# The row of -M of each head is written to DRAM and read back by transfers that GpSimd issues instead of SyncE

## The chip, the cores and the metric

The kernel runs on one core of one Trainium2 chip. The metric is the device time of one execution in microseconds (us). The profile names the engines PE (TensorE), PEld (its weight loads), DVE (VectorE), ACT (ScalarE), POOL (GpSimd) and SP (SyncE, which only issues transfers here). Its page shows two queues for the kernel's own transfers: q1, "hardware_dynamic", and q0, "software_dynamic". The transfers that SP issues run on the first, those that POOL issues on the second.

## The reference

One decoder layer on a sequence of 256 tokens and 1024 channels, in float32. A combined projection feeds two branches, an mLSTM branch (4 heads of 256) and an attention branch (8 heads of 128 with a relative position bias). The gated sum of both goes through an output projection, a LayerNorm, a convolutional gated MLP and a second LayerNorm. What matters here is the mLSTM branch, which weighs the scores of a head by exponentials that a running maximum keeps in range:

```python
log_f = jax.nn.log_sigmoid(f_pre.astype(jnp.float32))
b_cum = jnp.cumsum(chunks(log_f), axis=-1)
...
d_intra = jnp.where(causal, b_c[..., :, None] - b_c[..., None, :] + li_c[..., None, :], -jnp.inf)
m_q = jnp.maximum(inter, d_intra.max(-1))
...
s = jnp.einsum("bhld,bhsd->bhls", q_c, k_c) * jnp.exp(d_intra - m_q[..., None])
num = w_inter[..., None] * jnp.einsum("bhld,bhde->bhle", q_c, C) + jnp.einsum("bhls,bhse->bhle", s, v_c)
```

The kernel treats all 256 tokens as one chunk. With F the running sum of the log forget gates, G = (input gate) - F and M the running maximum of G, the weight of key s for query l is exp(G[s] - M[l]). G[s] is one number per partition there, and M[l] a row that all 128 partitions need.

## The kernel before

All weights pass through as 81 chunks of 1 MB (`order`). A chunk is loaded by SP into one of three `raw` buffers (line 94). ACT casts it to the high half `wh` (line 99), DVE takes the difference as the low half `wl` (line 100), and TensorE forms each product from three matmuls on the halves (lines 130 to 132). Step s of the loop in `run` first does the elementwise work of the step before and splits chunk s+2 (`elem_work`), then issues the load of chunk s+5, then the matmuls of chunk s, and then the small matmuls of the heads (`side_pe`). Every engine executes its instructions in the order in which this program issues them, and SP and POOL issue transfers in that order too: a transfer that has to wait holds back all that stands behind it on its engine.

Four groups g of eight steps each (qm, qb, km, kb, vm, vb, ga, gb) hold one mLSTM head and two attention heads. The gates of all four heads are worked out once, in group 0 (`gates_schedule`). At its end `e1d` puts -M of the four heads into `nM` (4 partitions of 256 numbers) and writes it to the DRAM tile `mrows`. In each group `row_m` reads the row of its head back to all 128 partitions, as `nMb`. The exponentials of `el_w` (lines 643 and 644, on ACT) read `nMb`; POOL then zeroes what is not causal (line 645), `el_s` multiplies with the scores and splits the product into `sph` (line 656, ACT) and `spl` (line 662, DVE), and `pe_n` multiplies these with the values into `psn`. In the table of the group's steps `row_m` stands in step 4, `el_w` in step 6 and `pe_n` behind the matmuls of step 6 (3, 5 and 5 in the last group).

POOL also issues the transfers of the attention bias. The table of biases is written to DRAM once (line 542). For each group `copy_band` (line 377) spreads two rows of it to a `band` in DRAM and `load_band` (line 382) reads that back, shifted by one number per partition, as `toe`.

Of the kernel before, what the change touches and what calls it, by code (L numbers as in the profile page):

```python
# [18 lines left out]
P = 128  # L19
S = 256  # L20
# [58 lines left out]
class Kernel:  # L79
# [469 lines left out]
    def gates_schedule(self, bif):  # L549
        nc, mp = self.nc, self.xp  # L550
        st = {}
        v = nc.vector

        def e0():
            gt = mp.tile([P, 2, 8], F32, name="gt")
            for t in range(2):
                v.tensor_add(gt[:, t, :], self.psg[t][:, 256:264], bif)
            st["gt"] = gt

        def p0():  # L560
            ps = self.ps_side([4, 2, S], "ps_gt")
            for w in range(2):
                for t in range(2):
                    nc.tensor.transpose(ps[:, w, t * P:(t + 1) * P], st["gt"][:, t, 4 * w:4 * w + 4], self.ident)
            st["ps"] = ps

        def e1():
            ps = st["ps"]
            big = mp.tile([P, KT, S], F32, tag="xraw", name="gates")
            fs, t1, F, G, M, nFM, nM = (big[0:4, k, :] for k in range(7))  # L570
            v.tensor_copy(fs, ps[:, 1, :])
            v.scalar_tensor_tensor(t1, fs, -1.0, fs, op0=ALU.mult, op1=ALU.min)
            nc.scalar.activation(t1, t1, AF.Exp)
            nc.scalar.activation(t1, t1, AF.Ln, bias=1.0)
            st["g"] = fs, t1, F, G, M, nFM, nM

        def e1b():
            fs, t1, F, G, M, nFM, nM = st["g"]
            one = self.ones4[:, 0:S]
            v.scalar_tensor_tensor(fs, fs, 0.0, t1, op0=ALU.min, op1=ALU.subtract)  # L580
            v.tensor_tensor_scan(F, one, fs, 0.0, op0=ALU.mult, op1=ALU.add)

        def e1c():
            fs, t1, F, G, M, nFM, nM = st["g"]
            v.tensor_sub(G, st["ps"][:, 0, :], F)
            v.tensor_tensor_scan(M, self.ones4[:, S:2 * S], G, 0.0, op0=ALU.max, op1=ALU.max)

        def e1d():
            fs, t1, F, G, M, nFM, nM = st["g"]
            v.tensor_scalar(self.nM[0:4, :], M, -1.0, None, op0=ALU.mult)  # L590
            v.scalar_tensor_tensor(nFM, F, -1.0, M, op0=ALU.mult, op1=ALU.subtract)
            st.update(G=G, nFM=nFM)
            nc.sync.dma_start(self.mrows, self.nM[0:4, :])

        def p1():
            ps = self.ps_side([P, 2, 2, 4], "ps_gc")
            for w, n in enumerate(("G", "nFM")):
                for t in range(2):
                    nc.tensor.transpose(ps[:, w, t, :], st[n][:, t * P:(t + 1) * P], self.ident[0:4, 0:4])
            st["gc"] = ps  # L600

        def e2():
            self.gcol = self.const.tile([P, 2, 4], F32, name="gcol")
            self.floor = self.const.tile([P, 2, 4], F32, name="floor")
            nc.scalar.copy(self.gcol, st["gc"][:, 0])
            self.floor_exp = lambda: nc.scalar.activation(self.floor, st["gc"][:, 1], AF.Exp)

        b = self.start_g[0]
        self.gate_sums = e0
        self.side_pe.setdefault(b, []).append(p0)  # L610
        self.mixed[b + 1] = lambda w: w[0:1] + [None, None] + w[1:] + [e1]
        self.mixed[b + 2] = lambda w: w + [e1b, None, e1c, None, e1d]
        self.side_pe.setdefault(b + 5, []).append(p1)
        self.gate_cols = e2


    def group_schedule(self, g):
        nc = self.nc
# [2 lines left out]
        b = self.start_g[g]  # L621

        def row_m():
            nc.sync.dma_start(self.nMb, self.mrows[g:g + 1, :].to_broadcast([P, S]))

        def pe_s():
            qh, ql = self.hl["qm"]
# [176 lines left out]

        o = int(g < NG - 1)
        at(self.side_elem, 3 + o, row_m)
        at(self.side_pe, 4 + o, pe_s)
        at(self.side_pe, 4 + o, lambda: pe_l(0))
# [411 lines left out]
```

## Time and profile before

| what | value |
|---|---|
| median of 3 runs | 487.28 us (487.03 to 487.93) |
| profiled execution, its own time | 487.25 us |
| span of its profile | 485.5 us (1.75 us lie around it) |
| PE busy | 476.1 us, 98% of the span |
| DVE, ACT, POOL busy | 76%, 59%, 6% |
| queue of SP (q1) | 87.61 MB, 50.7% of 16 DMA engines' span |
| queue of POOL (q0) | 6.07 MB, 3.8% |

Times in the profile count from the start of the span. A row of the timeline or of the chain begins with the start and the duration in us. The chain is followed back from the last instruction: at each step to what released it. A row of a wait reads "engine line waited for: us in total, times, longest". A row on a transfer ends with the us from its issue to its landing (the median, where it stands for several).

### The profile page before, as it was taken

The page shows a single profiled execution, that of the slowest core. Times are in us where ns is not written, and L with a number is a line of the kernel's source. Part 1 is how long each engine was busy: PE and PEld are TensorE (multiplying, and loading weights), DVE is VectorE, ACT ScalarE, POOL GpSimd, SP SyncE. Part 2 cuts the span into 40 slices and gives each one's busy share as a digit, 9 for nine tenths or more (in the row PEclk, how much of TensorE's full clock was granted, in tenths as well). Part 3 has the DMA queues.
Part 4 walks back from the last instruction along what each step waited for, and adds up shares of the span by engine and source line. Part 5 has one row for each costly group of instructions (what it writes and reads, how often), then busy time and mean ns, then how long its engine had stood idle before and what let it go on. Part 6 is the DMA issues. An engine that isn't in the chain of part 4 may idle for free.

```text
span 485.5 us, 9409 instructions
## 1 busy us (share of the span) xinstructions
PE 476.1 (98%) x3832; PEld 460.4 (95%) x3832; DVE 369.7 (76%) x674; ACT 287.1 (59%) x492; POOL 28.0 (6%) x43
## 2 busy tenths in 40 slices
PE   8999999999999999999999999999999999999993
PEld 6999999999999999999999999999999999999983
DVE  4877976797689668986677788888668666866877
ACT  5568775686667756866654622767456544654530
POOL 0501011001100110002000001000000000000000
PEclk9999999999999999999999999999999999999998
DMA  7985676375636552743954581727564655455202
GB/s 220 323 297 165 234 250 199 110 259 199 215 102 258 191 211 88 270 175 104 381 211 173 177 344 50 298 88 261 174 217 172 210 184 198 165 217 200 88 1 88
DMA packets 20918, 94.29 MB, mean 194 GB/s; under 512 B 4837, under 2 KB 7793, under 8 KB 11017
## 3 DMA queue, kind: packets, MB, share of 16 engines
q1 hardware_dynamic: 16714, 87.61, 50.7%
q0 software_dynamic: 4160, 6.07, 3.8%
q8 instruction: 30, 0.49, 0.4%
q14 instruction: 14, 0.11, 0.1%
HBM read 92.58 MB, written 2.64 MB: 196 GB/s over the span
## 4 chain that ended last, share of the span: by engine, by line
PE 84%; DMA 6%; DVE 6%; ACT 2%; issue 1%; SPq 1%; DVEq 0%; ACTq 0%
PE ps_up L132 8%; PE ps_up L131 8%; PE ps_up L130 8%; PE ffn L132 4%; PE ffn L131 4%; PE ffn L130 4%; DMA raw<-in_wst_dram 3%; DVE wl L100 3%; DMA nMb<-mrows 2%; PE mix L130 2%; PE ps_wa L131 2%; PE ps_wb L131 2%; PE ps_gb L132 1%; PE ps_gb L130 1%; PE ps_gb L131 1%; PE mix L132 1%
## 5 line engine op out<-in xcount | busy, mean ns | idle before, releaser
L100 DVE TENSOR_TENSOR wl<-raw,wh 128x1024 fp32r<-128x1024 f32 (+3 forms) x158 | 180.6, 1184 | 28.0 <-ACT wh L99 27.3
L99 ACT CAST wh<-raw 128x1024 fp32r<-128x1024 f32 (+3 forms) x158 | 152.5, 1018 | 9.2 <-DMA raw<-in_wst_dram 6.5
L132 PE MATMUL ps_up<-x1h,wl 128*128 128x256 f32 x320 | 88.6, 277 | 0.0
L130 PE MATMUL ps_up<-x1h,wh 128*128 128x256 f32 x320 | 88.6, 277 | 0.0
L131 PE MATMUL ps_up<-x1l,wh 128*128 128x256 f32 x320 | 88.5, 277 | 0.0
L131 PEld LDWEIGHTS ps_up<-x1l,wh 128*128 128x128 f32 x320 | 60.1, 188 | 0.4
L130 PEld LDWEIGHTS ps_up<-x1h,wh 128*128 128x128 f32 x320 | 60.1, 188 | 0.3
L132 PEld LDWEIGHTS ps_up<-x1h,wl 128*128 128x128 f32 x320 | 60.1, 188 | 0.0
L1045 DVE SCALAR_TENSOR_TENSOR cu<-ps_up,vec,cu 128x255 f32<-128x255 f32 (+1 forms) x80 | 33.0, 475 | 23.5 <-ACT cu L1041 23.5
L132 PE MATMUL ffn<-wh,hl 128*128 128x512 f32 (+1 forms) x94 | 35.5, 378 | 0.0
L131 PE MATMUL ffn<-wl,hh 128*128 128x512 f32 (+1 forms) x94 | 35.5, 377 | 0.0
L130 PE MATMUL ffn<-wh,hh 128*128 128x512 f32 (+1 forms) x94 | 35.3, 375 | 0.0
L99 ACT CAST hh<-cu 128x256 fp32r<-128x256 f32 x22 | 8.9, 406 | 42.9 <-DVE cu L1053 42.9
L1041 ACT ACTIVATE cu<-ps_up,vec 128x256 f32<-128x256 f32 x40 | 16.7, 468 | 26.1 <-PE ps_up L132 26.1
L132 PEld LDWEIGHTS ffn<-wh,hl 128*128 128x128 f32 x94 | 17.7, 188 | 3.2
L131 PEld LDWEIGHTS ffn<-wl,hh 128*128 128x128 f32 x94 | 17.7, 188 | 3.1
L130 PEld LDWEIGHTS ffn<-wh,hh 128*128 128x128 f32 x94 | 17.7, 188 | 3.0
L130 PE MATMUL ps_ga<-xth,wh 128*128 128x256 f32 x64 | 18.2, 284 | 0.0
L130 PE MATMUL ps_qm<-xth,wh 128*128 128x256 f32 x64 | 18.1, 282 | 0.0
L132 PE MATMUL ps_ga<-xth,wl 128*128 128x256 f32 x64 | 17.9, 280 | 0.0
L131 PE MATMUL ps_ga<-xtl,wh 128*128 128x256 f32 x64 | 17.9, 280 | 0.0
L130 PE MATMUL mix<-wh,mgh 128*128 128x256 f32 x64 | 17.9, 279 | 0.0
(319 smaller groups left out, 1438.7 us busy)
## 6 DMA issues: line engine op xcount, KB each, us to landing
raw<-in_wst_dram SPq DMA_DIRECT2D x77, 1024.0 KB, 4.9
raw<-in_wst_dram SPq DMA_DIRECT2D x8, 256.0 KB, 4.5
lnrow<-in_rows_dram POOLq DMA_DIRECT2D x4, 512.0 KB, 6.9
band<-table POOLq DMA_DIRECT2D x4, 384.0 KB, 13.5
xraw<-in_xt_dram SPq DMA_DIRECT2D x8, 128.0 KB, 3.9
toe<-band POOLq DMA_DIRECT2D x4, 256.0 KB, 4.8
xtok<-in_x_dram POOLq DMA_DIRECT2D x1, 1024.0 KB, 7.7
sgb<-in_wst_dram SPq DMA_DIRECT2D x4, 128.0 KB, 3.9
```

Of the source, the lines that this page charges most:

```text
L99: self.nc.scalar.copy(wh, raw)
L100: self.nc.vector.tensor_sub(wl, raw, wh.bitcast(F32))
L130: mm(ps, ah if first is None else first, bh, start=start, stop=False)
L131: mm(ps, ah, bl, start=False, stop=False)
L132: mm(ps, al, bh, start=False, stop=stop)
L1041: act.activation(cu[:, j, :], ps[:, j, :], AF.Copy, scale=tap(2, j))
L1045: v.scalar_tensor_tensor(cu[:, j, o:], ps[:, j, :S - o], tap(t, j), cu[:, j, o:], op0=ALU.mult, op1=ALU.add)
```

## The change

Two lines change: the write of `mrows` in `e1d` and the read of `nMb` in `row_m` are issued by POOL in place of SP. That is one write of 4 KB and four reads that each fill 128 KB. Where they stand in the program stays the same.

```diff
@@ -590,7 +590,7 @@
             v.tensor_scalar(self.nM[0:4, :], M, -1.0, None, op0=ALU.mult)
             v.scalar_tensor_tensor(nFM, F, -1.0, M, op0=ALU.mult, op1=ALU.subtract)
             st.update(G=G, nFM=nFM)
-            nc.sync.dma_start(self.mrows, self.nM[0:4, :])
+            nc.gpsimd.dma_start(self.mrows, self.nM[0:4, :])
 
@@ -621,7 +621,7 @@
         def row_m():
-            nc.sync.dma_start(self.nMb, self.mrows[g:g + 1, :].to_broadcast([P, S]))
+            nc.gpsimd.dma_start(self.nMb, self.mrows[g:g + 1, :].to_broadcast([P, S]))
```

The order on PE, DVE and ACT is the same. On POOL, this is what stands in group 0 between the first `toe` and the first causal selection (`wt_882` is the tile of weights of head 0):

```order
 L377 DMA band_411<-table 256x1x384
 L382 DMA toe<-band_411 128x2x256
+L593 DMA mrows<-nM 4x256
+L624 DMA nMb<-mrows 128x256
 L645 AFFINE_SELECT wt_882<-wt_882 128x256
 L377 DMA band_412<-table 256x1x384
```

The write and the first read now stand directly behind the load of `toe`, which itself waits for the band.

On POOL in group 1 (the other groups are alike; `scl_990` is a scale of head 0):

```order
 L704 TENSOR_TENSOR scl_990<-scl_990,mhalf 128x2
 L382 DMA toe<-band_412 128x2x256
+L624 DMA nMb<-mrows 128x256
 L645 AFFINE_SELECT wt_1513<-wt_1513 128x256
 L377 DMA band_413<-table 256x1x384
```

The read of the next head's row now follows the next `toe`.

On SP in group 0, where the `raw` are the weight chunks:

```order
 L94 DMA raw_447<-in_wst_dram 128x2048
 L94 DMA raw_529<-in_wst_dram 128x2048
-L593 DMA mrows<-nM 4x256
 L94 DMA raw_599<-in_wst_dram 128x2048
 L94 DMA raw_672<-in_wst_dram 128x2048
-L624 DMA nMb<-mrows 128x256
 L94 DMA raw_736<-in_wst_dram 128x2048
 L94 DMA raw_797<-in_wst_dram 128x2048
```

The write leaves its place two chunks ahead of the read, and the read its place behind chunk `raw_672`.

## Rows read from the trace of the kernel before

**Rows 1.** The page: the span, and TensorE's busy time.
```profile
span 485.5 us, 9409 instructions
PE 476.1 (98%) x3832; PEld 460.4 (95%) x3832; DVE 369.7 (76%) x674; ACT 287.1 (59%) x492; POOL 28.0 (6%) x43
```
**Rows 2.** Waits, of PE from 29 to 235 us and of ACT from 46 to 92.
```profile
PE psn L132 <- DVE spl L662: 0.3, 1, 0.3
...
ACT L643 <- DMA nMb<-mrows: 0.9, 1, 0.9
```
**Rows 3.** The chain that ended last, from 56 to 72 us.
```profile
57.84 0.33 SPq L94
...
58.22 7.87 DMA nMb<-mrows
...
66.18 1.28 ACT L643
...
71.58 0.39 PE psn L132
```
**Rows 4.** Timeline of SP.
```profile
52.33 0.28 SPq L593 DMA_DIRECT2D mrows<-nM  x1
```
**Rows 5.** Timeline of POOL, groups 0 and 1 (in brackets idle time, and what ended it).
```profile
38.15 0.54 POOL L542 DMA_DIRECT2D table<-ev  x1 [18.64 <-DVE cvqm L441]
43.13 1.12 POOL L377 DMA_DIRECT2D band<-table  x1 [4.44 <-DMA table<-ev]
57.07 0.77 POOL L382 DMA_DIRECT2D toe<-band  x1 [12.81 <-DMA band<-table]
68.41 0.41 POOL L645 TENSOR_SCALAR_AFFINE_SELECT wt<-wt 128x256 f32<-128x256 f32 x1 [10.58 <-ACT wt L644]
...
83.14 0.90 POOL L382 DMA_DIRECT2D toe<-band  x1 [0.90 <-DMA band<-table]
```
**Rows 6.** Transfers issued from 57 to 59 us.
```profile
raw<-in_wst_dram SPq DMA_DIRECT2D x1, 1024.0 KB, 7.9
toe<-band POOLq DMA_DIRECT2D x1, 256.0 KB, 7.4
```
**Rows 7.** Timeline of POOL from 228 us, and transfers issued at 229.9 to 230.5.
```profile
229.43 0.74 POOL L833 DMA_DIRECT2D xtok<-in_x_dram  x1 [8.70 <-PE pso L785]
230.16 1.10 POOL L843 DMA_DIRECT2D lnrow<-in_rows_dram  x2
...
xtok<-in_x_dram POOLq DMA_DIRECT2D x1, 1024.0 KB, 7.7
lnrow<-in_rows_dram POOLq DMA_DIRECT2D x1, 512.0 KB, 8.4
```
**Rows 8.** The four `toe` loads, the write of the bias table, two stores of the output.
```profile
DMA to landing us min/median/max: 3.7/4.8/7.4
...
table<-ev POOLq DMA_DIRECT2D x1, 12.0 KB, 4.7
...
out_dram<-r SPq DMA_DIRECT2D x2, 256.0 KB, 2.0
```
**Rows 9.** Timeline of ACT, group 1.
```profile
113.93 0.41 ACT L643 ACTIVATE wt<-nMb,gcol 128x128 f32<-128x128 f32 x1
```
**Rows 10.** Stretches at the end: busy time of PE, PEld, DVE, ACT, POOL, then PE's granted clock.
```profile
478.00:480.00 2.00, 0.08 (x1) 0.00 (x0) 1.78 (x6) 0.00 (x0) 0.40 (x1) 1.00 0.01 4
480.00:482.00 2.00, 0.00 (x0) 0.00 (x0) 2.00 (x5) 0.00 (x0) 0.25 (x1) 0.76 0.00 0
482.00:484.00 2.00, 0.00 (x0) 0.00 (x0) 0.36 (x1) 0.00 (x0) 0.00 (x0) 0.50 0.73 262
```
**Rows 11.** Timeline of PE at the start.
```profile
1.25 3.60 PE L183 MATMUL warm_ps<-warm 128*128 128x512 bf16 x8 [1.25 <-DVE warm L180]
...
5.28 0.41 PE L403 MATMUL ps_o2b<-wh,xtl 128*128 128x256 f32 x1
...
6.84 0.40 PE L403 MATMUL ps_o0b<-wh,xth 128*128 128x512 f32 x1
```

## Prediction

> **What bounds the kernel now.** I read the page first. TensorE is busy for 476.1 of 485.5 us [rows 1], so a change of two transfers can only matter where TensorE waits. The list of TensorE's waits comes next: between 29 and 235 us, the stretch in which the gates and the four groups run, it holds one row, 0.3 us before a matmul of `psn` that waits for `spl` [rows 2]. Nothing else stops TensorE there; weight chunks are always ready in time.
>
> The third view is the chain around that wait [rows 3], and it leads straight to the transfers that the change moves. In group 0 SP issues a weight chunk at 57.84 and the read of `nMb` behind it at 58.22. The row lands 7.87 us later, at 66.09. ACT has by then waited 0.9 us for it [rows 2], so it was free at about 65.28. From there the work is serial: a table load at 66.18, the exponentials, the evacuations that stand between them and the scores, `sph`, `spl`, and the matmul that waited, at 71.58. That is 5.5 us from the landing of `nMb` to TensorE, with 0.3 us of idle TensorE at the end of it. So in group 0 the landing of `nMb` sets TensorE's time one for one: each us later is a us of idle TensorE, and no later slack gives it back, since TensorE is busy without a wait through the groups that follow. Earlier is worth almost nothing: at most the 0.3 us that TensorE waits.
>
> The fourth view is POOL's timeline, since POOL is where the transfers go [rows 5]. POOL is nearly idle, but in group 0 its one instruction at the time in question, the load of `toe`, waits 12.81 us for the band and is issued only from 57.07 to 57.84.
>
> **The change part by part.**
>
> *The write.* On SP it is issued at 52.33, as soon as `nM` is there [rows 4]. On POOL it stands behind the load of `toe`, so it can't be issued before 57.84: 5.5 us later, by the order of the queue alone. SP loses an instruction on which it sat waiting, and the weight chunk behind it can go out a few tenths of a us earlier. I cost that at nothing, because TensorE waits for no chunk in the stretch; if that cover were gone, the change would still only move the chunk forward.
>
> *When the write has landed.* The read must wait for that. Before, this wait was hidden: 5.9 us lay between the two issues on SP (52.33 to 58.22), and the read went out right behind the chunk. Now they stand next to each other, and the whole of the write's latency is on the chain. The trace doesn't show this write's landing, so I bound it. The lower bound is the store of the output at the quiet end of the run, 2.0 us [rows 8]. A nearer row is the write of the bias table on the same queue: issued at 38.15, its reader on POOL starts at 43.13, 4.98 us from issue to issue [rows 5], of which 4.7 are its landing [rows 8] and 0.28 the start of the reader. But that write found the queue of POOL empty. This one stands behind `toe`, which takes 7.4 us to land [rows 6], that is until 64.47, because it runs against a weight chunk that itself takes 7.9. The trace shows twice that transfers of one queue land in the order of issue, the later just behind the earlier: `nMb` on SP's queue lands at 66.09 and the chunk ahead of it at 57.84 + 7.9 = 65.7 [rows 3, 6], though `nMb` is an eighth of its size; on POOL's queue `xtok`, issued at 229.43, lands at 237.1, and the first `lnrow` behind it, issued at 230.16, at 238.6 [rows 7]. So I take the landing of `toe` plus the 0.35 us that separated chunk and `nMb`: 64.8. With 0.28 us the read starts at 65.1. An upper bound for the start is a further 2.0 us (a write that only begins when `toe` has landed), 66.8.
>
> The Trainium skill speaks to this in "DMA: Bandwidth & Descriptors", section "Why a DMA increments its semaphore by 16 and not by 1": on the software path all 16 engines post the completion, whatever the shape of the transfer. By that even a write of four rows is complete only when the slowest of the 16 rings has got past its share of `toe`, which is the case that I took; no row shows it for a transfer this small.
>
> *The read.* Its issue on POOL is part of what a landing time counts. The nearest rows are the `toe` loads on the same queue, twice its bytes: 3.7 us at best, 4.8 in the median, 7.4 in the slot just described [rows 8]. The read of 65.1 falls between: the chunk issued at 57.84 has landed, later chunks are under way. I take 4.8. It lands at 65.1 + 4.8 = 69.9, against 66.09 before: **+3.8 us**. From the bounds: earliest 65.1 + 3.7 = 68.8 (+2.7), latest 66.8 + 7.4 = 74.2 (+8.1), the latter with two worst cases at once; 65.1 + 7.4 = 72.5 (+6.4) is the end that I keep.
>
> *What waits meanwhile.* ACT stands at the table load of `el_w` with everything behind it; DVE soon waits for ACT; POOL's next instruction is the causal selection, which already waited 10.58 us for ACT [rows 5], so POOL's new wait holds nothing up. TensorE finishes the matmuls of step 6 and stands before `psn`. All of it moves by the same 3.8 us.
>
> *Groups 1 to 3.* Their reads move too, from SP to directly behind the next `toe` on POOL. In group 1 that `toe` is issued at 83.14 [rows 5] and the exponential that needs the row runs at 113.93 [rows 9]. Even with two landings of 7.4 us one after the other the row is there by 99. I cost these three at nothing; the cover is at least 14 us of other steps, and the last two groups have the same order.
>
> *Sum.* 487.25 + 3.8 = **491.1 us**. The profiled execution lies 0.03 us below the median of the runs, so the comparison with 487.28 is the same.
>
> **The rivals.**
>
> *A. TensorE's clock falls in the longer wait.* At the end of the run TensorE does its last work at 478.08; the granted clock is 1.00 until 480, 0.76 in the next 2 us and 0.50 after that [rows 10]. If 0.76 is a mix of 2.4 and 1.2 GHz, the fall came at about 481.0, after 2.9 us of idleness. The wait that I forecast is 0.3 + 3.8 = 4.1 us, so this can happen here. The way back can be read at the start: from its first matmul at 1.25 TensorE was busy, and yet at 5.28 a matmul of 256 columns took 0.41 us, as long as one of 512 columns at 6.84 [rows 11]. So at most 5.6 us at half speed, which loses at most 2.8. The wait is near the length at which the fall showed, and the loss lies between 0 and 2.8, so I take half: 491.1 + 1.4 = 492.5.
>
> The skill's "TensorE: Matmul & The Clock Gate", in its section "The HAM clock gate", says too that an idle TensorE drops to half rate and earns the full rate back by being busy. No run here shows yet whether a stall inside the kernel does it.
>
> *B. The write does not queue behind `toe`.* Then the bias table's 4.98 us are the price: the read starts at 57.84 + 4.98 = 62.8 and lands 3.7 to 5.7 us later (5.7 lies midway between the best and the worst `toe`, rounded up), at 66.5 to 68.5: +0.4 to +2.4, about 488.6. For it speaks that 4 KB is little; against it the two ordered landings above.
>
> *C. Not slower: both transfers take their quiet time.* 57.84 + 2.0 + 0.28 + 3.7 = 63.8, before ACT is free at 65.28. Then ACT's wait of 0.9 us and TensorE's of 0.3 vanish, and the time is 487.25 - 0.3 = 486.9. It decides if the write lands within 4.3 us of its issue (66.09 - 3.7 - 0.28 - 57.84) and the read at its best. Against it: the same stretch gave `toe` 7.4 and the chunk 7.9.
>
> The skill would come out here: "DMA: Bandwidth & Descriptors", section "Anatomy of one DMA", gives about 2.0 us plus the bytes at 436 GB/s for a transfer on this path. An estimate by it is 57.84 + 2.0 + 0.28 + 2.3 = 62.4 for the landing. By that rule no time is lost; the trace disagrees for the transfer just ahead on the same queue, whose 256 KB took 7.4 us.
>
> **How the numbers follow.** A change within 0.2%, that is between 486.3 and 488.25 us, can't be told from none with this kernel. My chances: the forecast with the clock held 0.53 (489.9 to 493.7); with A 0.27 (490 to 496.5); B 0.12, a third of it within 0.2%; C 0.06; something that I don't see and that makes it faster 0.02. So faster 0.02, same 0.06 + 0.04 = 0.10, slower 0.88. The range leaves out C, the lower part of B, and above it the worst landings with a fallen clock: 488.2 to 494.2.
>
> **What would show it.** In the changed profile POOL issues `mrows` at about 57.8 and `nMb` at about 65; ACT's wait at line 643 is 4 to 5 us in place of 0.9; TensorE's wait before `psn` in group 0 is about 4 us, and no such wait stands in groups 1 to 3. If `nMb` is issued at 62 to 63, B holds and the ordered landing was the wrong step. If it is issued at 65 and lands in under 3 us, the read was priced too high. A granted clock of 0.5 behind the wait shows A. A wait of TensorE in a later group, or for a weight chunk, would be something that I have not seen.

## The result, and the profile after

| kernel | median | executions | ratio |
|---|---|---|---|
| before | 487.23 us (486.34 to 488.68) | 22 | |
| changed | 489.63 us (487.59 to 493.01) | 22 | 1.0056, 95% interval 1.0041 to 1.0071 |

The change makes the kernel slower, by 2.4 us in the median and by 2.7 us in the mean, which the ratio follows. The median describes few executions, though. The 22 times of the changed kernel in order:

```
487.59 487.69 487.82 487.86 487.88 488.05 488.07 488.16 488.16 488.42
489.37 489.89 490.40 490.66
492.02 492.54 492.72 492.76 492.76 492.82 492.83 493.01
```

Ten lie some 0.7 us above the median of before, eight some 5.5 us above it, four between. In what follows the ten are the short executions and those of 491 us and more the long ones. The kernel before has no such split. The profiled execution took 489.37 us. First the span, the busy time and all waits of TensorE of the changed kernel:

```profile
span 487.7 us, 9413 instructions
PE 477.7 (98%) x3832; PEld 461.8 (95%) x3832; DVE 370.6 (76%) x674; ACT 287.6 (59%) x492; POOL 31.2 (6%) x48
...
PE warm_ps L183 <- DVE warm L180: 1.2, 1, 1.2
PE ps_o0a L403 <- ACT wh L99: 0.5, 1, 0.5
```

The wait before `psn` is not there at all, not even the 0.3 us of [rows 2]. So this execution is one in which the change cost TensorE nothing in group 0. POOL's timeline of it, and the transfers that were issued from 57.3 to 62 us, are the counterparts of [rows 5] and [rows 6]:

```profile
56.62 0.77 POOL L382 DMA_DIRECT2D toe<-band  x1 [12.10 <-DMA band<-table]
57.38 0.53 POOL L593 DMA_DIRECT2D mrows<-nM  x1
60.92 0.59 POOL L624 DMA_DIRECT2D nMb<-mrows  x1 [3.00 <-DMA mrows<-nM]
...
toe<-band POOLq DMA_DIRECT2D x1, 256.0 KB, 3.6
nMb<-mrows POOLq DMA_DIRECT2D x1, 128.0 KB, 3.3
mrows<-nM POOLq DMA_DIRECT2D x1, 4.0 KB, 3.0
```

The order is the one forecast: the write directly behind `toe`, the read only when the write has landed, and the write lands (57.38 + 3.0 = 60.4) just behind `toe` (56.62 + 3.6 = 60.2). But `toe` took 3.6 us here and not the 7.4 of [rows 6], and the read 3.3. It landed at 64.2, before ACT was ready for it at 66.0. Why this execution is still 2.1 us above the median of before has two other causes. The first is the start. The matmul of 512 columns that took 0.40 us at 6.84 before [rows 11] took 0.63 us here, and the shorter durations came only at about 10.5. The fourth matmul on `ps_o2a` therefore began 1.9 us later. The first row is of the kernel before, the other two of the changed one, all from PE's timeline:

```profile
8.74 0.29 PE L403 MATMUL ps_o2a<-wh,xth 128*128 128x256 f32 x1
```
```profile
7.21 0.63 PE L403 MATMUL ps_o0b<-wh,xth 128*128 128x512 f32 x1
...
10.63 0.29 PE L403 MATMUL ps_o2a<-wh,xth 128*128 128x256 f32 x1
```

These durations point to TensorE's lower clock. But the granted clock reads 1.00 in this stretch of both traces, so only the durations speak for it. In all later traces of the changed kernel the fourth matmul began at 8.6 to 8.9, so the late start does not belong to the change. The second cause is at the end of the run, and is told with the experiments.

### The profile page after: what moved, and what is told of

Same layout as the page of the kernel before. It is cut to its first block, busy times and chain, and to the rows that moved or that the text cites. A ratio compares the mean times of both kernels' runs of the same rounds, so it can differ in the third digit from the quotient of the medians.

```text
span 487.7 us, 9413 instructions
## 1 busy us (share of the span) xinstructions
PE 477.7 (98%) x3832; PEld 461.8 (95%) x3832; DVE 370.6 (76%) x674; ACT 287.6 (59%) x492; POOL 31.2 (6%) x48
## 4 chain that ended last, share of the span: by engine, by line
PE 97%; DMA 1%; DVE 1%; issue 0%; SPq 0%; ACT 0%; DVEq 0%
PE ps_up L132 8%; PE ps_up L130 8%; PE ps_up L131 8%; PE ffn L132 4%; PE ffn L131 4%; PE ffn L130 4%; PE ps_ga L131 2%; PE ps_qm L130 2%; PE ps_ga L132 2%; PE ps_ga L130 2%; PE ps_vb L132 2%; PE ps_vb L130 2%; PE ps_vb L131 1%; PE ps_wb L132 1%; PE ps_vm L130 1%; PE ps_kb L131 1%
## 5 line engine op out<-in xcount | busy, mean ns | idle before, releaser
L945 POOL TENSOR_TENSOR rs<-rs,mhalf 128x1 f32<-128x1 f32 x4 | 2.8, 692 | 243.1 <-DVE rs L944 243.1
```

The source lines that it names most:

```text
L945: nc.gpsimd.tensor_tensor(st["rs"], st["rs"], self.mhalf[:, 0:1], op=ALU.pow)
```

## The experiments

The theory after this result: the order of the queue is as forecast, but the landings of the band, of `toe`, of the write and of the read differ from execution to execution. When the read lands before ACT is ready, nothing is lost; when it lands later, TensorE waits. The rival: the long executions have another cause (the start, the later groups, weight chunks).

**The changed kernel again, four more traces** (no edit).

> The changed kernel once more, for a second trace and more times. Landing theory: in each execution the read of group 0 lands where the traffic of that moment lets it, between 64 and 71 us, while ACT is ready for it at about 65 to 66; so an execution is as fast as before (487 to 488.4) if it lands in time, and 3 to 6 us slower if it doesn't, with TensorE waiting before psn by the difference. If this trace is of a time above 490, TensorE waits 2 us or more before psn in group 0; if it is below 489, it waits 0. Rival, that the slow executions come from elsewhere (the start, later groups, weight chunks): a trace above 490 shows no wait before psn.

> The changed kernel, one more trace, to catch one of the executions above 489.8 us (11 of 34 so far). Landing theory: if it is one, the write or the read of group 0 lands late (read after 67), TensorE waits before psn by the same time, and the granted clock is 0.5 for some us behind a wait of over 3 us. Rival (the time goes elsewhere): no such wait in a trace above 490.

> As for the run before: a trace above 490 us shows by landing theory a read that lands after 67 us and TensorE waiting before psn; by the rival it shows neither. A trace below 489 shows no wait by both.

> As for the run before: a trace above 490 us shows by landing theory a read that lands after 67 us and TensorE waiting before psn; by the rival it shows neither. A trace below 489 shows no wait by both.

The first gave 487.94 us in the median (487.45 to 494.48, 12 executions, ten of them up to 488.68 and two above 492.8; ratio 1.0032, interval 1.0003 to 1.0060), with a trace at 487.92. The single ones gave 491.47, 487.56 and 492.44. So two of the single traces caught a long execution. POOL's timeline and TensorE's waits at 491.47 us:

```profile
57.97 0.77 POOL L382 DMA_DIRECT2D toe<-band  x1 [14.30 <-DMA band<-table]
58.73 0.53 POOL L593 DMA_DIRECT2D mrows<-nM  x1
63.52 0.59 POOL L624 DMA_DIRECT2D nMb<-mrows  x1 [4.25 <-DMA mrows<-nM]
...
PE psn L130 <- ACT sph L656: 1.6, 1, 1.6
...
PE psn L132 <- DVE spl L662: 0.3, 1, 0.3
```

The same at 492.44 us:

```profile
57.84 0.77 POOL L382 DMA_DIRECT2D toe<-band  x1 [13.38 <-DMA band<-table]
58.60 0.53 POOL L593 DMA_DIRECT2D mrows<-nM  x1
64.37 0.59 POOL L624 DMA_DIRECT2D nMb<-mrows  x1 [5.24 <-DMA mrows<-nM]
...
PE psn L130 <- ACT sph L656: 2.1, 1, 2.1
...
PE psn L132 <- DVE spl L662: 0.3, 1, 0.3
```

And at 487.56 us, with no wait of TensorE before `psn`:

```profile
56.02 0.77 POOL L382 DMA_DIRECT2D toe<-band  x1 [12.10 <-DMA band<-table]
56.79 0.53 POOL L593 DMA_DIRECT2D mrows<-nM  x1
60.28 0.59 POOL L624 DMA_DIRECT2D nMb<-mrows  x1 [2.96 <-DMA mrows<-nM]
```

The difference begins at the band: `toe` is issued 1.8 to 2.0 us later, since the band landed later. Then the write takes 4.2 and 5.2 us in place of 2.9, and the read is issued 3.2 and 4.1 us later. ACT's timeline shows what that did, first at 491.47, then at 492.44 us:

```profile
67.97 1.28 ACT L643 ACT_TABLE_LOAD   x1 [3.30 <-DMA nMb<-mrows]
```
```profile
69.08 1.28 ACT L643 ACT_TABLE_LOAD   x1 [3.50 <-DMA nMb<-mrows]
```

The rival falls: both traced long executions show the wait, and where it was forecast. Behind it stands a second loss. Stretches of the first (busy time of PE, PEld, DVE, ACT, POOL, then the granted clock):

```profile
71.00:74.00 3.00, 1.14 (x7) 0.93 (x8) 1.92 (x6) 3.00 (x9) 0.87 (x1) 1.00 0.15 22
74.00:78.00 4.00, 4.00 (x23) 4.00 (x23) 3.96 (x17) 1.76 (x7) 0.00 (x0) 0.57 0.56 74
78.00:82.00 4.00, 4.00 (x36) 4.00 (x36) 3.91 (x9) 2.25 (x4) 0.00 (x0) 1.00 0.60 242
```

and of the second:

```profile
74.00:78.00 4.00, 3.66 (x20) 3.53 (x19) 3.77 (x10) 1.76 (x3) 0.00 (x0) 0.57 0.28 56
78.00:82.00 4.00, 4.00 (x36) 4.00 (x36) 3.93 (x19) 3.36 (x8) 0.00 (x0) 1.00 0.91 258
```

TensorE was busy for 1.14 of 3 us around the wait, and in the next 4 us its granted clock (the share of the full 2.4 GHz) was 0.57, mostly 1.2 GHz: 23 matmuls where the 4 us after hold 36. To split the loss, the execution at 487.92 can be laid beside that at 491.47, since both started alike (the matmul on `ps_rel` at 28.61 and 28.58). The stalled matmul of `psn` started at 71.45 in the one and 73.37 in the other: 1.9 us of waiting. In the chain that ended last, the first `pst` started at 77.91 and 81.65: 3.7 us, of which the remaining 1.8 fell in the stretch of the low clock. From there to the start of the last matmul both take the same time (399.8 and 399.7 us).

**Only the reads on GpSimd.**

```diff
-            nc.sync.dma_start(self.nMb, self.mrows[g:g + 1, :].to_broadcast([P, S]))
+            nc.gpsimd.dma_start(self.nMb, self.mrows[g:g + 1, :].to_broadcast([P, S]))
```

> Only the four reads are issued by GpSimd, the write stays on SyncE at 52 us. Landing theory: the write has landed before the load of toe is issued, so the read goes out at about 57.5 directly behind it and lands at 62 to 65.5; TensorE never waits before psn, all times in one cluster, median 486.4 to 487.4 (0 to 0.6 us faster than before). Rival, that the reads on the GpSimd queue cost by themselves (queueing behind toe, later groups): times as of the changed kernel, median 488 to 490, some near 492.8.

Measured: 487.52 us (487.16 to 488.98, 12 executions; ratio 1.0005, 0.9994 to 1.0017), with no second group of long times. POOL's timeline:

```profile
56.78 0.77 POOL L382 DMA_DIRECT2D toe<-band  x1 [12.27 <-DMA band<-table]
57.54 0.57 POOL L624 DMA_DIRECT2D nMb<-mrows  x1
```

The read goes out directly behind `toe`, took 5.9 us and landed at 63.4; TensorE did not wait. The long executions are gone. The median is a little above what the theory gave (486.4 to 487.4).

**Only the write on GpSimd.**

```diff
-            nc.sync.dma_start(self.mrows, self.nM[0:4, :])
+            nc.gpsimd.dma_start(self.mrows, self.nM[0:4, :])
```

> Only the write is issued by GpSimd, behind toe at about 57; the reads stay on SyncE. Landing theory: SyncE waits for the write's landing (60 to 65) before it issues the read, so the read lands at 64 to 71 as in the changed kernel, and the same mixture of times appears, median 488 to 491, some above 492. The weight chunks queued behind the read on SyncE are late too when the write lands after 62. Rival, that the reads cost: median as before, 487.2.

Measured: 487.78 us (486.77 to 491.60, 12 executions; ratio 1.0024, 1.0006 to 1.0043), with three times from 490.24 up. SP's timeline shows that the read, which here goes out 1.8 us ahead of the next weight chunk, now waits for the write, issued at 57.98 and landed 3.0 us later:

```profile
60.95 0.33 SPq L624 DMA_DIRECT2D nMb<-mrows  x1
62.72 4.92 SPq L94 DMA_DIRECT2D raw<-in_wst_dram  x2
```

So with the write alone behind `toe` times above 490 are back, 3 of 12, though none reached 492 as I had expected of some. The trace is of a short execution, in which TensorE did not wait before `psn`; that the three lost their time in that wait is inferred, not shown. The chunk behind the read was not held up in this trace.

**Both on GpSimd, ahead of the load of `toe` in group 0.**

```diff
@@ rel_bias_expand
             self.copy_band(0)
-            self.load_band(0)
@@ group_schedule
         at(self.side_elem, 3 + o, row_m)
+        if g == 0:
+            at(self.side_elem, 3 + o, lambda: self.load_band(0))
```

> Both on GpSimd, but in group 0 the write and the read are issued ahead of the load of toe. Theory that the place behind toe is what costs: the write goes out at about 52.5, the read at 56, and it lands at 60 to 62; no wait of TensorE before psn, all times in one cluster, median 486.4 to 487.4. Rival, that the two transfers back to back on that queue cost wherever they stand: median 488 or more, some above 492.

Measured: 487.85 us (487.33 to 488.88, 12 executions; ratio 1.0012, 1.0002 to 1.0022), none above 489. The median is above the 486.4 to 487.4 that I expected, and the times inside were not the expected ones either. POOL's timeline, and the transfers by their landing:

```profile
52.79 0.66 POOL L592 DMA_DIRECT2D mrows<-nM  x1 [8.51 <-DVE nM L589]
57.99 0.59 POOL L623 DMA_DIRECT2D nMb<-mrows  x1 [4.54 <-DMA mrows<-nM]
58.57 0.74 POOL L382 DMA_DIRECT2D toe<-band  x1
...
mrows<-nM POOLq DMA_DIRECT2D x1, 4.0 KB, 4.9
...
band<-table POOLq DMA_DIRECT2D x1, 384.0 KB, 13.9
```

The write was issued at 52.79 and landed only at 57.7, 0.6 us behind the band (43.16 + 13.9 = 57.1), which was then the transfer ahead of it on the queue. The read went out 2 us later than I expected, landed 5.5 us later at 63.5 and was still in time.

**One transfer more in the chain**, and the same with TensorE kept busy.

```diff
             nc.gpsimd.dma_start(self.mrows, self.nM[0:4, :])
+            nc.gpsimd.dma_start(self.mrows2, self.mrows)
...
-            nc.gpsimd.dma_start(self.nMb, self.mrows[g:g + 1, :].to_broadcast([P, S]))
+            nc.gpsimd.dma_start(self.nMb, self.mrows2[g:g + 1, :].to_broadcast([P, S]))
```

> The changed kernel with one more transfer in the chain of group 0: mrows is copied to a second DRAM tile, and the reads are made from that. All three are issued by GpSimd behind toe. It adds one more issue and landing, 3 to 5 us. Landing theory: from the traces without a wait (read landed at 64.2 and 65.4, ACT ready at about 65.9) the read now lands at 67.5 to 70 and nearly every execution stalls: TensorE waits 2 to 4.5 us before psn, the time is 489.5 to 492.5 in most runs, and about 1.5 us more where the wait is over 3 us long and the granted clock falls to 0.5. Rival, that the slow executions of the changed kernel are not due to this chain: median 487.5 to 488.5 as in the fast cluster, with the same share near 492.8.

Measured: 491.01, 492.46, 494.14 and 495.94 us (ratio 1.0144, 1.0112 to 1.0176). No short execution is left, so the length of this chain does set the time; two of the four lie above the 492.5 that I expected of most, and no trace of those two was taken. In the trace, at 491.01, the read is issued at 63.82, lands 5.2 later at 69.0, and TensorE waits:

```profile
PE psn L130 <- ACT sph L658: 2.2, 1, 2.2
...
74.00:76.00 2.00, 1.66 (x13) 1.45 (x13) 1.81 (x4) 1.65 (x2) 0.00 (x0) 1.00 0.27 47
76.00:78.00 2.00, 2.00 (x20) 2.00 (x19) 1.97 (x7) 0.11 (x1) 0.00 (x0) 1.00 0.13 46
```

The wait is as long as in the two long executions above, and the clock held at 1.00 this time, although from 71 to 74 us TensorE was busy for only 0.82 us, against 1.14 and 0.92 in the long ones. So neither the length of the wait nor the idleness of that stretch tells the two cases apart; what does was not found.

```diff
+            for _ in range(20 if g == 0 else 0):
+                nc.tensor.matmul(n0[:, 0:S], self.hl["qm"][0][:, 0, 0:P], self.hl["km"][0][:, 0, :], start=True, stop=True)
             self.mm3(n0, sph[:, 1, :], spl[:, 1, :], vh[:, 0, :], vl[:, 0, :], True, True)
```

> The kernel with the extra transfer in the chain, and 20 matmuls of 256 columns (2.3 us at full clock) put before the first psn of group 0, so that TensorE has work while it waits; their result is overwritten. If the loss beyond the wait is the clock: the wait before psn shrinks by about 2.3 us (to 0 to 2), the granted clock stays at 1.00 behind it, and the times are at most those of the unfilled kernel without a fall, 490.5 to 492, with none above 493.5. If the clock has no part in the loss, the times stay as without the filling, 491 to 496.

Measured: 491.46, 491.92, 495.67 and 496.04 us (ratio 1.0131, 1.0096 to 1.0167). In the trace, at 491.92, the read landed at 69.5 and TensorE's wait is 0.8 us, with the clock at 1.00 behind it:

```profile
PE psn L130 <- ACT sph L658: 0.8, 1, 0.8
...
76.00:78.00 2.00, 2.00 (x19) 2.00 (x18) 2.00 (x5) 0.15 (x1) 0.00 (x0) 1.00 0.12 46
```

Two of the four times are above 493.5, which I had expected of none; as a set they are what I had expected if the clock had no part in the loss (491 to 496). The trace is of one of the two shorter ones, so what the two above 495 lost can't be told. This experiment doesn't settle the clock's part.

**The read of group 0 one chunk earlier, on SyncE; and groups 1 to 3 alone on GpSimd.**

```diff
-        at(self.side_elem, 3 + o, row_m)
+        at(self.side_elem, 3 + o - (g == 0), row_m)
```

> The kernel before, with one move: in group 0 SyncE issues the read of nMb one weight chunk earlier, so that it no longer lands behind that chunk. Theory that TensorE's 0.3 to 0.6 us before psn in the kernel before come from this landing: the read goes out at 55 to 56 and lands by 63, ACT and TensorE don't wait, and the time falls by 0.3 to 0.6 us (0.05 to 0.12%), median 486.7 to 487.0. Rival, that removing this wait brings nothing (as in the run with only the reads on GpSimd): 487.2 to 487.5.

Measured: 487.23 us (486.51 to 488.55, 12 executions; ratio 1.0000, 0.9991 to 1.0010). The read was issued at 56.37 and landed 3.2 us later; TensorE did not wait, and the time did not fall as I had expected; in the second trace of the kernel before, below, that wait is not there either.

```diff
-            nc.sync.dma_start(self.nMb, self.mrows[g:g + 1, :].to_broadcast([P, S]))
+            (nc.gpsimd if g else nc.sync).dma_start(self.nMb, self.mrows[g:g + 1, :].to_broadcast([P, S]))
```

> Group 0 as in the kernel before (write and first read on SyncE), the reads of groups 1 to 3 on GpSimd. Theory that only group 0 counts: times as of the kernel before, one cluster, median 487.1 to 487.5, no time above 489.5. Rival, that transfers on the GpSimd queue cost something in the later groups or at the end: 0.5 us or more above before, or some times above 490.

Measured: 487.70 us (487.17 to 489.28, 12 executions; ratio 1.0012, 1.0002 to 1.0023). No execution is long, so it is group 0 that splits the times. But the median is 0.7 us above the 486.95 of the kernel before that ran beside it, which is the rival's figure (0.5 us or more). The trace has no wait of TensorE before `psn` or in groups 1 to 3; its end, as told below, is some 0.5 us longer, and the rest of the 0.7 is not explained.

**The kernel before, once more** (no edit).

> The kernel before, a second trace, to see what varies from run to run without the change. Theory: the band lands between 56 and 58 here too, but the read of nMb went out at 58.2 in any case, so TensorE's wait before psn stays under 1 us. Rival, that the kernel before has waits of 2 us there too: one shows, and the time is above 489.

Measured: 486.96 us. `toe` landed in 3.4 us and TensorE did not wait before `psn`. The 7.4 us of [rows 6] and the 0.3 us of [rows 2] are not fixed properties of the kernel before either.

**What the traces say together.** `toe` is the transfer whose landing the forecast rested on. Over the 14 traces it goes with how far ahead of the weight chunk of that moment it is issued:

```
lead over the chunk (us)   landing of toe (us)   traces
1.2 to 2.2                 3.4 to 4.2            9
1.0                        4.3                   only the reads on GpSimd
0.8                        7.4                   before
0.3                        5.8                   changed, 492.44
-0.5                       6.0                   ahead of toe
-0.7                       4.8                   changed, 491.47
```

With 1.2 us or more of lead `toe` was quick in every trace. Below that it was slower, but not in the order of the lead, and no run moved the chunk alone: the link is a correlation.

The end of the run explains the 0.7 us that executions without a wait lose. From the end of SP's last output store issue to the end of the span it is 2.7 to 2.8 us in the three traces with all transfers on SP, and 3.1 to 3.5 in the other eleven. Rows of SP in the kernel before (span 485.5) and in the changed one at 487.92 us (span 486.2): the stores, and SP's twelve semaphore instructions of the program's end (line 1216, with the start of the first and the last):

```profile
481.46 1.35 SPq L1112 DMA_DIRECT2D out_dram<-r  x3
...
L1216 SPq EVENT_SEMAPHORE  x12: 17/28/28, 482.9 to 485.5; - x12
```
```profile
481.42 1.36 SPq L1112 DMA_DIRECT2D out_dram<-r  x3
...
L1216 SPq EVENT_SEMAPHORE  x12: 17/28/28, 482.8 to 486.2; - x12
```

The stores are issued at the same time, and the span ends 0.7 us later (485.5 - 482.81 = 2.7 against 486.2 - 482.78 = 3.4). It is not the stores: in all 14 traces the last one lands 1.6 to 1.7 us after the end of its issue. What grows is the time from that landing to the end of the span: 1.05 us with no transfer moved off SP, 1.44 with one, 1.58 with three, 1.66 with four, 1.8 with five.

The traces' records of the semaphores show what stands there. The transfers that SP issues signal their landing on eight semaphores in turn (100, 101, 103, 104, 106, 107, 108, 109). At the end SP tests them one after another, always in this order, 0.06 to 0.09 us apart. With all transfers on SP the last store has the semaphore 107, and the tests of those before it are done while the stores are still under way; each transfer that is moved off SP shifts the turn by one, so the last store has 106 with one moved, 103 with three, 101 with four and 100 with five. Behind its landing 2, 3, 5, 6 and 7 semaphores are then left to test. Once among SP's instructions behind the landing there is also a pause of about 0.35 us in the eleven traces, and none in the three; what it is was not found. So the 0.7 us hang on how many transfers SP issues, not on POOL's queue. By the same turn a sixth transfer moved would give the last store 109, with none of the eight left to test behind it; no run tried that.

## Why the prediction came out as it did

- **Group 0 sets the time, and the landing of `nMb` passes to TensorE one for one.** Right. In the execution at 491.47 the read landed at 67.8 (63.52 + 4.3), the matmul of `psn` that waits for `spl` followed 5.5 us later (73.37), as in [rows 3], and no later stretch gave anything back. That groups 1 to 3 cost TensorE nothing was right too: no trace has a wait there.
- **The write queues behind `toe` and lands just behind it.** Right, and closer than forecast: in the five traces of the changed kernel it landed 0.2 us behind `toe`, whether `toe` took 3.5 or 5.8. Rival B falls. That the place in the queue is the cause is shown by the runs that change it: with the write on SP, or ahead of `toe`, none of 12 executions each is above 489, where 12 of 37 of the changed kernel are long. The run with only the write on POOL, 3 of 12 above 490, fits.
- **`toe` lands at 64.5.** Wrong in size, and this is the term of the sum that failed. I took 7.4 us from one execution and called it the price of the slot. In five traces of the changed kernel `toe` took 3.5 to 5.8 us and landed at 59.5 to 63.6. With the write behind it the read started at 60.3 to 64.4 instead of 65.1.
- **The read takes 4.8 us.** 3.3 to 4.7 in the five traces, so a little too much, by a few tenths in the long executions.
- **Sum.** +3.8 us for every execution was forecast. Of the 37 executions of the changed kernel in this study 21 took up to 488.7 us, 12 took 491.4 or more, 4 lay between. The two traces of the 21 have no wait before `psn` and lose only what the end of the run adds. So the commonest case is what I called rival C and gave 0.06: landings early enough, though its 486.9 missed the 0.7 us at the end. My 491.1 lies between the two cases, where no execution was found, and the median falls near it only because the mixture puts it between them too. That is luck. It is luck as well that the long executions come near it: TensorE waits 1.9 and 2.4 us in them and not the 4.1 of the forecast, and 1.65 to 1.8 us behind the wait and 0.7 at the end, which are not in the sum, make up for it.
- **Rival A, the clock.** It happens: 0.57 granted for 4 us in both long traces, 1.65 to 1.8 us lost (in the one at 492.44: 4.7 later at `pst` than at 487.92, less 0.6 from the start and 2.45 of waiting). I had priced it at 1.4 and put the fall at about 2.9 us of idleness; it came with waits of 1.6 and 2.1 us, each followed by one of 0.3. In the trace with one more transfer it did not come with waits of 2.2 and 0.3. Nor are 5.6 us from the first matmul a bound for the way back: in the changed trace at 489.37 the long durations lasted to about 10.5.
- **Not foreseen:** 0.7 us at the end of the run, from the shifted turn of the completion semaphores.

What stays open: why the band lands anywhere between 55.7 and 57.7 us, when the clock falls behind a wait, what lies between 488.7 and 491.4 (the one trace from there is the late start), and what the executions of 494 to 496 us lost, of which there is no trace.

## What to carry to other kernels

A transfer's landing read from one trace is one draw. Before it becomes a term of a sum, look at how near it stands to other traffic, and ask what the sum gives at its best landing as well: here a hand-off that looked late by 4 us was in time, as far as the times show it, in over half of the executions. A write and its read through DRAM belong on a queue where nothing large, and nothing that itself waits, stands ahead of the write, because in these traces a 4 KB write landed 0.2 us after the `toe` ahead of it, whenever that was. Where TensorE is the bound, a wait of 2 us can cost 4, since the clock may fall behind it. And a transfer that changes its queue also changes which completion semaphore each later transfer of the old queue has: a constant loss of some tenths of a us can come from the end of the program, far from the change.

## What was not expected of the hardware

- The end of the run grew with the number of transfers moved off SP: 2.7 to 2.8 us from the last store's issue to the end of the span with none moved, 3.1 to 3.3 with one or three, 3.3 with four, 3.4 to 3.5 with five. The last store's completion semaphore comes earlier in SP's closing series of tests, and more of them are left when it lands.
- The granted clock fell to 0.57 in the mean of 4 us behind a wait of 1.6 us that was followed by one of 0.3, and held at 1.00 behind waits of 2.2 and 0.3.
- At the start, TensorE's matmuls had the longer durations up to about 10.5 us in one of five traces of the same kernel, against about 6 in the other four. That alone cost 1.9 us, 0.4% of the time.
